# One more x tile of block 1 transposed by DMA instead of TensorE, and one cast of the head in two halves

## The chip, the core and the metric

The kernel runs on one core of a Trainium2 chip. A core has TensorE (PE; its weight loads are shown as PEld), VectorE (DVE), ScalarE (ACT), GpSimd (POOL) and SyncE (SP), which run their own instruction streams and wait for each other by semaphores, and 16 DMA engines. The metric is the device time of one execution in microseconds (us).

## The reference

x is 16 x 512 x 768, w1 768 x 3072, b1 3072, w2 3072 x 768, all float32. What is computed:

```
y = np.matmul(x, w1) + b1
y = 0.5 * y * (1.0 + erf(y / np.sqrt(2.0)))
return np.matmul(y, w2)
```

## The kernel before

**Tiling.** The 8192 rows of x are cut into eight blocks (sb) of 1024 rows; a block has 8 row tiles t of 128 rows. The first product runs with the 768 (k) on the partitions, so a block's x is needed transposed: `XTs[sb]` holds, for row half a (0: tiles 0 to 3, 1: tiles 4 to 7) and k chunk c (0 to 5), 128 x 512 values in fp16. Both products use a 2x2 Strassen-Winograd scheme with seven products p1 to p7. For the first one A11 and A12 are the lower and upper three k chunks of row half 0, and A21 and A22 those of row half 1. The sums of x (`x_sums`, L321) are S1 = A21 + A22 (k = 0), S2 = S1 - A11 (k = 1), then A11 - A21 (k = 2) and A12 - S2 (k = 3), all on DVE.

**Units and periods.** A unit of the first product, `Unit1` for (sb, k), makes 256 of the 3072 hidden values for one block: seven products of three matmuls of 512 columns, 21 matmuls. `period(i, j, fill)` (L666) interleaves unit i with the end of unit j before it: p1(i) into bank bX and its copy to bY (`copy_xy`, ACT, L606); p7(j) into bY and an add on DVE (L613); p5(i) into bW and a copy (ACT, L626); p3(j) into bZ and an add (DVE, L641); p6(i) into bY, and a copy of bY to bZ (for block 0 and even units of block 1 on DVE, L659); right_done(j), a GELU on ACT (L404); p4(j) into bY and its GELU (ACT, L409); p2(i) into bX and its GELU (ACT, L409). Banks bX and bY exist twice, bW and bZ once. Between these calls `fill(slot)` is called with slots 1 to 6, and hangs in the work beside the matmuls: loads, sums, transposes.

**The order of units** at the start is written out by hand in `seq` (L818): units 0 to 6 of block 0, then (1,0), (1,1), (1,2), (0,7) and so on. A unit's place in it is `pos`. The first two are computed in the head with plain matmuls.

**The head** (L713 to L816). SP loads x tiles 0 to 3 of block 0 in float32, then the first two column chunks of w1 in two halves (L723). For each of the four tiles DVE casts it to fp16 (L746), PE transposes six 128 x 128 pieces into the bank bT (`transpose_pe`, L311, the transposes are L313), ACT copies them to XTs[0] (L315; for tile 3 in two halves, `copy_halves`, L307, L309), and some dummy matmuls (`spin`, L737) follow. DVE then casts the w1 chunks in three instructions (L754: two of 384 columns from the first half, one of 768 from the second), and the plain matmuls (L762) begin: three into bX and three into bY with the lower k chunks, then the same with the upper ones.

**x of block 1.** POOL loads its eight tiles with a cast to fp16 (`load_next_x`, L824, issued at L299), in the order 0, 4, 1, 5, 2, 6, 3, 7, between loads of weight tiles 4, 5 and 6 (L222). `transposes_a(pos)` (L850), called in slot 5 of pos 1 to 4, transposes tiles pos - 1 and pos + 3 by DMA on SP's queue (`transpose_dma`, L304), but not those in `X1_PE` (L845), which `fill_a` (L855) transposes on PE in a slot of a pos given by `X1_AT` (L846): tile 3 in slot 2 of pos 5, tile 7 in slot 1 of pos 6. In slot 5 of pos 7, SP stores the weight tiles 0 to 6 with their sums to DRAM (`keep`, L224, issued at L225, times in `KEEP`, L848), behind the transposes on the same queue. The sums of x of block 1 are queued at pos 5 (columns 0 to 255 of k = 0, 1), pos 6 (columns 256 to 511 of k = 0, 1) and pos 7 (k = 2, 3); unit (1,0), at pos 7, is the first to use XTs[1]. `prep_wt` (L227) queues the sums of a weight tile on DVE for the unit behind; all these sums run at L191.

Of the kernel before, what the change touches and what calls it, by code (L numbers as in the profile page):

```python
# [10 lines left out]
P = 128  # L11
# [11 lines left out]
def kernel(  # L23
# [8 lines left out]
    nc = tc.nc  # L32
    B, M, K = x.shape
# [6 lines left out]
    KQ = K // P // 2  # L40
# [48 lines left out]
    def cut(off, n, pattern=None, **dims):  # L89
        ap = arena[:, off:off + n]  # L90
        return ap.rearrange(pattern, **dims) if pattern else ap
# [94 lines left out]
    with tc.manual_schedule():  # L186
# [103 lines left out]
        xhs = {}  # L290

        def xh_of(sb, t):
            if sb < ONE:
                return cut(sb * GR + GR // 2 + t * K, K)
            return xh_late[t % 3]
# [8 lines left out]
        def transpose_dma(sb, t):  # L304
            nc.sync.dma_start_transpose(out=xT_of(sb, t), in_=xhs[t])

        def copy_halves(out, in_):  # L307
            for c in (slice(0, KQ), slice(KQ, 2 * KQ)):
                nc.scalar.copy(out=out[:, c, :], in_=in_[:, c, :])  # L309

        def transpose_pe(sb, t, copy=nc.scalar.copy):  # L311
            for kc in range(2 * KQ):
                nc.tensor.transpose(out=bT[t % 2][:, kc, :], in_=xhs[t][:, kc * P:(kc + 1) * P],  # L313
                                    identity=ident[:])
            copy(out=xT_of(sb, t), in_=bT[t % 2][:])  # L315
# [397 lines left out]
        xf = cut(GR, 8 * K).bitcast(FP32).rearrange("p (t k) -> p t k", t=4)  # L713
# [23 lines left out]
        def spin(n):  # L737

            for k in range(n):
                nc.tensor.matmul(out=(bX[1], bY[1])[k % 2][:], lhsT=zero[:, 0, 0:P], rhs=zero[:, 0, :],  # L740
                                 start=True, stop=True, skip_group_check=True)

        spin(9)
        for t in range(4):
            xhs[t] = xh_of(0, t)
            nc.vector.tensor_copy(out=xhs[t], in_=xf[:, t, :])  # L746
            transpose_pe(0, t, copy_halves if t == 3 else nc.scalar.copy)
            if t == 0:
                nc.tensor.transpose(out=bW[:, 0:2 * NH], in_=bf, identity=idf[0:2 * NH, 0:2 * NH])
                nc.scalar.copy(out=b1t[:], in_=bW[:, 0:2 * NH])  # L750
            spin(2)
# [15 lines left out]
        def plain_done(n, row, side):  # L767
            nc.scalar.activation(out=Gs[0][side][:, n, row, :], in_=banks[n, row][side][:, 0:RH],
                                 func=GELU, bias=b1t[:, 2 * n + side:2 * n + side + 1])
# [72 lines left out]
            if pos in w2_at_pos:  # L842
                load_w2(*w2_at_pos[pos])

        X1_PE = (3, 7)  # L845
        X1_AT = ((5, 2), (6, 1))  # L846

        KEEP = {at[1, 0]: range(7), at[0, 7] + 1: (7,), at[0, 8]: (8,), at[0, 9]: (9,), at[0, 10]: (10,), at[0, 11]: (11,)}  # L848

        def transposes_a(pos):  # L850
            for t in (pos - 1, pos + 3):
                if t not in X1_PE:
                    transpose_dma(1, t)

        def fill_a(pos, slot):  # L855
            if pos == 2 and slot == 1:
                plain(1, 1, 1, 1, bottom)
                plain_done(1, 1, 1)
            if (pos, slot) in X1_AT:
                transpose_pe(1, X1_PE[X1_AT.index((pos, slot))])  # L860
            if pos == at[1, 0] - 1 and slot == 2:
# [267 lines left out]
```

## Time and profile before

| what | value |
|---|---|
| median of 4 runs | 853.23 us (852.84 to 853.58) |
| the profiled execution | 853.01 us, span 851.2 us |
| granted TensorE clock | 1.0 |
| PE busy | 844.6 us, 99% of the span |
| DVE, ACT, POOL busy | 78%, 49%, 10% |
| transposes on PE (L313) | 60: six for each of the eight tiles of block 0 and of tiles 3 and 7 of block 1 |
| DMA transposes on SP (L305) | 54, six of them for block 1 |

The span runs from the first to the last instruction of the program; the execution's own time has 1.8 us more around it. A line of the timeline gives the start and the length in us, the engine, the line of the code, the operation with what it writes and reads, the number of merged instructions, and in brackets the idle time of the engine just before it with what ended it. A matmul's length contains its drain, which the next one overlaps; starts tell the rate. A DMA's line on SP is the time of its issue, not of the transfer; the time from issue to landing is a figure of its own. Line numbers are those of the program above.

### The profile page before, as it was taken

The page shows a single profiled execution, that of the slowest core. Times are in us where ns is not written, and L with a number is a line of the kernel's source. Part 1 is how long each engine was busy: PE and PEld are TensorE (multiplying, and loading weights), DVE is VectorE, ACT ScalarE, POOL GpSimd, SP SyncE. Part 2 cuts the span into 40 slices and gives each one's busy share as a digit, 9 for nine tenths or more (in the row PEclk, how much of TensorE's full clock was granted, in tenths as well). Part 3 has the DMA queues.
Part 4 walks back from the last instruction along what each step waited for, and adds up shares of the span by engine and source line. Part 5 has one row for each costly group of instructions (what it writes and reads, how often), then busy time and mean ns, then how long its engine had stood idle before and what let it go on. Part 6 is the DMA issues. An engine that isn't in the chain of part 4 may idle for free.

```text
span 851.2 us, 16487 instructions
## 1 busy us (share of the span) xinstructions
PE 844.6 (99%) x6432; PEld 568.7 (67%) x6432; DVE 667.4 (78%) x1126; ACT 421.3 (49%) x686; POOL 83.8 (10%) x135
## 2 busy tenths in 40 slices
PE   8999999999999999999999999999999999999998
PEld 5444445687544897448974499645995469944798
DVE  4766678786657998579976799668996689956998
ACT  4777762122277512783148722487216771267611
POOL 5021100002100002000020000210002100010000
PEclk9999999999999999999999999999999999999999
DMA  9998687649999599987999689995999959984398
GB/s 224 193 277 187 159 167 255 256 190 221 231 326 216 191 324 369 319 166 234 341 365 299 130 286 333 362 269 136 318 342 342 285 120 331 352 310 173 100 309 285
DMA packets 143522, 219.05 MB, mean 257 GB/s; under 512 B 61756, under 2 KB 84724, under 8 KB 143444
## 3 DMA queue, kind: packets, MB, share of 16 engines
q1 hardware_dynamic: 117824, 179.74, 66.9%
q0 software_dynamic: 25440, 38.15, 20.6%
q8 instruction: 50, 0.82, 0.4%
q14 instruction: 28, 0.23, 0.1%
q10 hardware_dynamic: 180, 0.11, 0.0%
HBM read 180.30 MB, written 47.87 MB: 268 GB/s over the span
## 4 chain that ended last, share of the span: by engine, by line
PE 98%; DMA 1%; ACT 1%; DVE 0%; issue 0%; SPq 0%; ACTq 0%
PE bY L388 21%; PE bY L493 15%; PE bX L388 14%; PE bX L493 10%; PE bW L388 7%; PE bZ L388 7%; PE bZ L493 5%; PE bW L493 5%; PE bY L432 5%; PE bW L432 2%; PE bX L432 2%; PE bZ L432 2%; PE bY L580 1%; PE bX L580 1%; DMA arena<-in_x_dram 1%; PE bX L762 0%
## 5 line engine op out<-in xcount | busy, mean ns | idle before, releaser
L191 DVE TENSOR_TENSOR arena<-arena 128x768 f16<-128x768 f16 (+4 forms) x630 | 403.8, 672 | 8.1 <-PE bW L432 1.1
L388 PEld LDWEIGHTS <-arena 128*128 128x128 f16 x1974 | 192.5, 98 | 223.9
L493 PEld LDWEIGHTS <-arena 128*128 128x128 f16 x3528 | 292.1, 98 | 8.4 <-issue 0.4
L388 PE MATMUL bY<-arena 128*128 128x512 f16 x846 | 214.4, 379 | 0.0
L613 DVE TENSOR_TENSOR arena<-bY,arena 128x512 f32<-128x512 f32 (+1 forms) x102 | 69.4, 681 | 127.1 <-PE bY L388 90.4
L493 PE MATMUL bY<-arena 128*128 128x192 f16 x1500 | 138.3, 246 | 0.0
L388 PE MATMUL bX<-arena 128*128 128x512 f16 x564 | 138.2, 379 | 0.0
L606 ACT COPY bY<-bX 128x512 f32<-128x512 f32 (+1 forms) x143 | 78.6, 550 | 119.4 <-DVE arena L542 82.0
L404 ACT ACTIVATE arena<-arena,b1t 128x1024 f16<-128x1024 f32 x94 | 108.1, 1150 | 53.8 <-DVE arena L641 53.8
L626 ACT COPY arena<-bW 128x512 f32<-128x512 f32 (+1 forms) x147 | 81.1, 552 | 90.7 <-PE bW L493 43.9
L493 PE MATMUL bX<-arena 128*128 128x192 f16 x1020 | 93.1, 246 | 0.1
L641 DVE TENSOR_TENSOR arena<-bZ,arena 128x512 f32<-128x512 f32 (+1 forms) x102 | 69.3, 680 | 20.9 <-PE bZ L388 18.2
L388 PE MATMUL bW<-arena 128*128 128x512 f16 x282 | 76.2, 379 | 0.0
L388 PE MATMUL bZ<-arena 128*128 128x512 f16 x282 | 76.2, 379 | 0.0
L432 PEld LDWEIGHTS <-arena 128*128 128x128 f16 x528 | 51.6, 98 | 34.1 <-issue 0.2
L525 POOL DMA_DIRECT2D out_dram<-arena x42 | 30.6, 729 | 407.4 <-DVE arena L637 371.3
L409 ACT ACTIVATE arena<-bX,b1t 128x512 f16<-128x512 f32 x94 | 64.0, 681 | 10.0 <-PE bX L388 10.0
L409 ACT ACTIVATE arena<-bY,b1t 128x512 f16<-128x512 f32 x94 | 63.4, 674 | 0.0
L657 ACT COPY bZ<-bY 128x512 f32<-128x512 f32 (+1 forms) x54 | 29.0, 537 | 65.6 <-DVE arena L641 31.4
L299 POOL DMA_DIRECT2D arena<-in_x_dram x60 | 32.6, 550 | 248.1 <-DMA arena<-arena 139.3
L493 PE MATMUL bZ<-arena 128*128 128x192 f16 x504 | 48.4, 246 | 0.0
L493 PE MATMUL bW<-arena 128*128 128x192 f16 x504 | 48.4, 246 | 0.0
(60 smaller groups left out, 400.2 us busy)
## 6 DMA issues: line engine op xcount, KB each, us to landing
arena<-w2s SPq DMA_DIRECT2D x294, 288.0 KB, 4.7
arena<-w1s SPq DMA_DIRECT2D x72, 672.0 KB, 7.1
out_dram<-arena POOLq DMA_DIRECT2D x42, 384.0 KB, 7.4
w2s<-arena SPq DMA_DIRECT2D x49, 288.0 KB, 3.6
arena<-in_x_dram POOLq DMA_DIRECT2D x60, 192.0 KB, 7.0
w1s<-arena SPq DMA_DIRECT2D x12, 672.0 KB, 5.5
arena<-in_w_dram POOLq DMA_DIRECT2D x17, 384.0 KB, 8.8
out_dram<-arena SPq DMA_DIRECT2D x17, 384.0 KB, 3.6
```

The source lines that it names most:

```text
L191: nc.vector.tensor_tensor(out=o, in0=a, in1=b, op=op)
L299: nc.gpsimd.dma_start(out=xhs[t], in_=xr[:, sb * 8 + t, :])
L388: nc.tensor.matmul(out=dst[:, 0:RH], lhsT=w1_op(self.wt, slot)[:, c, :], rhs=a[:, c, :], start=first and c == 0, stop=c == self.C - 1, ski ...
L404: nc.scalar.activation(out=self.G[1][:, hi, :, :], in_=self.tmp, func=GELU, bias=b1t[:, 2 * hi + 1:2 * hi + 2])
L409: nc.scalar.activation(out=self.G[0][:, hi, row, :], in_=bank[:, 0:RH], func=GELU, bias=b1t[:, 2 * hi:2 * hi + 1])
L432: nc.tensor.matmul(out=dst[:, 0:N2], lhsT=a, rhs=w[:, :, c, :], start=first and c == 0, stop=c == self.C - 1, skip_group_check=True)
L493: nc.tensor.matmul(out=dst[:, t * N4:(t + 1) * N4], lhsT=a, rhs=w[:, c, :], start=first and c == 0 and t == ts[0], stop=c == NQ - 1, skip_ ...
L525: eng.dma_start(out=orr[:, s0:s0 + 2, right * N2:(right + 1) * N2], in_=self.dst[:, r].rearrange("p t h n -> p t (h n)"))
L606: nc.scalar.copy(out=bY[u.g % 2][:, 0:u.F], in_=bX[u.g % 2][:, 0:u.F])
L613: nc.vector.tensor_tensor(out=u.c22(), in0=bY[u.g % 2][:, 0:u.F], in1=w[:, 0:u.F], op=ADD)
L626: nc.scalar.copy(out=w[:, 0:u.F], in_=bW[:, 0:u.F])
L641: nc.vector.tensor_tensor(out=u.c12(), in0=bZ[:, 0:u.F], in1=w[:, 0:u.F], op=ADD)
```

## The change

The list of tiles that PE transposes for block 1 loses tile 3, which so goes to `transpose_dma` at pos 4, behind tile 6 and ahead of the keep stores. Tile 7 stays on PE, at the same place. In the head, the cast of x row tile 3 becomes two casts of 384 columns each; the transposes and the two half copies behind it are as before.

```diff
+        KH = KQ * P
...
         for t in range(4):
             xhs[t] = xh_of(0, t)
-            nc.vector.tensor_copy(out=xhs[t], in_=xf[:, t, :])
+            if t < 3:
+                nc.vector.tensor_copy(out=xhs[t], in_=xf[:, t, :])
+            else:
+                nc.vector.tensor_copy(out=xhs[t][:, 0:KH], in_=xf[:, t, 0:KH])
+                nc.vector.tensor_copy(out=xhs[t][:, KH:K], in_=xf[:, t, KH:K])
             transpose_pe(0, t, copy_halves if t == 3 else nc.scalar.copy)
...
-        X1_PE = (3, 7)
-        X1_AT = ((5, 2), (6, 1))
+        X1_PE = (7,)
+        X1_AT = ((6, 1),)
```

KQ is 3 and P is 128, so KH is 384.

## The prediction

> **What bounds the kernel now.** I read the page's busy table first, then the chain that ended last, then the timeline of the two places that the diff touches.
>
> ```profile
> PE 844.6 (99%) x6432; PEld 568.7 (67%) x6432; DVE 667.4 (78%) x1126; ACT 421.3 (49%) x686; POOL 83.8 (10%) x135
> ...
> PE 98%; DMA 1%; ACT 1%; DVE 0%; issue 0%; SPq 0%; ACTq 0%
> ```
>
> TensorE is busy for 844.6 of 851.2 us, and 98% of the chain is matmuls. Its idle time lies almost wholly in the first 10.4 us; behind that a wait of PE is a rare thing of 0.1 to 0.3 us. So work taken off PE is worth its time, unless an engine that was just in time before is now just too late. The whole question is which of those is near.
>
> **Part 1: the six transposes of tile 3 leave PE.** The timeline of units (0,5) and (0,6), PE alone:
>
> ```profile
> 35.12 0.81 PE L388 MATMUL bW<-arena 128*128 128x512 f16 x3
> 35.77 0.50 PE L313 MATMUL bT<-ident,arena 128*128 128x128 f16 x6
> 36.10 0.81 PE L388 MATMUL bZ<-arena 128*128 128x512 f16 x3
> ...
> 39.34 0.81 PE L388 MATMUL bY<-arena 128*128 128x512 f16 x3
> 39.99 0.50 PE L313 MATMUL bT<-ident,arena 128*128 128x128 f16 x6
> ```
>
> The columns are start, span, engine, line. Three matmuls of 512 columns take 0.65 us from start to start (35.12 to 35.77). The six transposes of tile 3 hold PE from 35.77 to 36.10: 0.33 us (the 0.50 counts the last one's drain, which the next matmul overlaps). Removed: 0.33 us of PE, and one ACT copy of 0.81 us (the bT copy at 36.47), which lies in 1.09 us of ACT's idle time and is worth nothing. The six for tile 7 (39.99) stay.
>
> What is late next? DVE, in the same stretch:
>
> ```profile
> 36.59 1.15 DVE L191 TENSOR_TENSOR arena<-arena 128x384 f16<-128x384 f16 x3 [0.51 <-DMA arena<-in_w_dram]
> 37.65 0.68 DVE L641 TENSOR_TENSOR arena<-bZ,arena 128x512 f32<-128x512 f32 x1
> 38.44 0.70 DVE L659 COPY bZ<-bY 128x512 f32<-128x512 f32 x1
> ```
>
> DVE waited until 36.59 for a load of w1 (weight tile 6, for prep_wt), not for PE. The three sums, L641 and the copy bZ<-bY (L659) follow without a gap, so the copy ends at 39.14 whether PE is earlier or not. Behind it waits p7 of unit (0,5), the matmuls into the same bY at 39.34: they overwrite what the copy reads. Elsewhere in this trace PE starts 0.05 us after such a copy (L654 ends at 302.48, PE goes on at 302.53). So p7 can start at 39.19, not at 39.34 - 0.33 = 39.01: of the 0.33 us **0.15 us stays** and 0.18 becomes a wait on DVE.
>
> Does the 0.15 us survive? ACT's chain L404, L409, L409, L606 starts at 38.37 from that L641 and does not move; L606, which p6 of (0,6) waits for, ends at 41.15, and PE wants it at 41.62 - 0.15 = 41.47. The copy of tile 7 stays at 41.08 to 41.89, so the sum S1 (k = 0 of x_sums, columns 256 to 511) stays at 41.92; it reads row block 1, tiles 4 to 7, and not tile 3. From there L641, L404, L409, L409 and L606 end at 45.91, PE could go on at 45.96, and p6 of (1,0) wants 46.15 - 0.15 = 46.00. It just fits. Behind that the waits shrink again, and the rest of the program is moved by 0.15 us as a whole.
>
> **Part 2: a seventh DMA transpose on SP.** It is issued behind that of tile 6 and ahead of keep(0):
>
> ```profile
> 36.84 1.24 SPq L305 DMA_TRANSPOSE arena<-arena  x1
> ...
> 38.17 2.39 SPq L225 DMA_DIRECT2D w1s<-arena  x1
> ```
>
> Its source, x tile 3, has landed by 32.5 (the trace's landing of that load), so it starts at 36.84 + 1.24, some 38.10. Added on SP: one issue of 1.2 us (median of L305: 1.228) to 5.7 us (the longest, for tile 1, with the queue full). The seven or eight keep stores queued behind it move by 1.2 to 2.4 us. The first one landed at 43.4 and its slot is reloaded at 51.1, when POOL is released by PE: 7.7 us of cover, so nothing.
>
> Tile 3 is due when PE starts p1 of unit (1,0), the first reader of A11: 43.56 - 0.15 = 43.41, so a landing by 43.36, which is 5.26 us after the issue. S2 (k = 1), its other reader, runs on DVE at 43.79 and is due only before p6. How long does a transpose take from issue to landing?
>
> ```profile
> DMA to landing us min/median/max: 2.7/5.3/10.9
> ```
>
> Bounds: 2.7 us (landing 40.8) and 10.9 us (49.0). I take the row next to it, tile 6, one place ahead in the same queue: 5.0 us, so 43.1, in time by 0.3 us. Two things say that this is rather too long. Tile 6 stood behind five others, and from about 38.5 to 40.9 the DMA engines moved next to nothing: the packet records have a 16 KB fetch of PE's instructions on queue q8 from 38.17 to 40.18, 2.0 us where most of its kind take 0.9 to 1.0, and the transposes stood still meanwhile. And nothing else loads the queues there: the last weight load landed at 36.56. With 12 PE instructions fewer (six weight loads, six matmuls) the fetch comes about 1 us later and may hold tile 3 instead: then it lands about 1.6 us after the fetch's end, as tile 6 did (40.18 to 41.79), so at 39.15 + 2.0 + 1.6 = 42.75. Still in time.
>
> The Trainium skill speaks against this part. Its page "VectorE: DVE Perf Modes", section "Rules for kernel authors", would transpose 128x128 on TensorE where PSUM will do as destination, and by DMA otherwise; section "The three transpose paths" prices one at 390 ns there and 1309 ns by DMA. An estimate by the page: six by DMA are 7.85 us, a landing at 45.95, and PE would lose about 2.4 us against before. The trace has 55 ns of PE for one transpose in a row of six and whole tiles landing in 2.7 us when undisturbed, so the sum goes by the trace.
>
> **Part 3: the cast of x row tile 3 in two halves.** The head's timeline:
>
> ```profile
> 8.36 0.92 DVE L746 CAST arena<-arena 128x768 f16<-128x768 f32 x1 [0.42 <-DMA arena<-in_x_dram]
> 9.49 0.80 DVE L754 CAST arena<-arena 128x384 f16<-128x384 f32 x2 [0.21 <-DMA arena<-in_w_dram]
> 11.08 0.56 DVE L754 CAST arena<-arena 128x768 f16<-128x768 f32 x1 [0.79 <-DMA arena<-in_w_dram]
> ...
> 10.41 0.81 PE L762 MATMUL bX<-arena 128*128 128x512 f16 x3
> 11.05 0.81 PE L762 MATMUL bY<-arena 128*128 128x512 f16 x3
> ...
> 11.70 0.81 PE L762 MATMUL bX<-arena 128*128 128x512 f16 x3
> ```
>
> The nearest rows for a half are the two w1 casts of 128x384, 0.47 and 0.40 us with starts 0.40 apart. The halves would end at about 8.8 and 9.23 (9.28 before). The last three transposes then start at 9.28 instead of running in a row of six from 9.34, and end at 9.62 instead of 9.84; ACT's first half copy, which began 0.04 after them, and the first matmul come 0.22 earlier, at 10.19. But the second half of these matmuls, at 11.70, reads the third w1 cast, which waits for its load until 11.08 and ends at 11.64; its weight load starts at 11.69. Before, PE was busy until that very moment; now it would be done at 11.48 and wait. **Worth 0.00 us**: the w1 load hides it. The bounds: 0.28 us gained, if that load came as much earlier (the first matmul can go no earlier than the first w1 cast at 9.96 lets it); and 0.92 us lost, if each half took as long as the whole cast, since the second half of the matmuls then moves to 12.62.
>
> **The sum.** 0.15 us off PE, 0 in the head, 0 for SP: the profiled execution goes from 853.01 to 852.86 us (its span from 851.2 to 851.1). The median of the four runs, 853.23, lies 0.22 above it, so I forecast **853.1 us**. A measurement of this kernel can tell about 0.2%, 1.7 us, from no change; this is a tenth of that.
>
> **The rivals.**
> - *The whole gain.* Speaks for it: DVE's late start hangs on one load's landing (36.56), and 0.18 us earlier would free all 0.33 us, 852.9 us; with the head's 0.28 as well, 852.6. Against: both loads are issued as before, with the same traffic beside them. Chance 0.17.
> - *The gain is eaten whole.* p6 of (1,0) fits by 0.04 us only; if the shifted fetch holds tile 6 so that S1 starts at 42.1 instead of 41.92, that chain ends at 46.15 and the time is 853.2. That the change does nothing looks the same. Chance 0.15.
> - *Tile 3 lands late: slower.* PE itself then waits, in front of p1 of (1,0), with everything queued behind it, and every microsecond counts in full. Break-even is a landing at 43.51, 5.4 us after the issue. For it: the median of this line is 5.3, and tile 2, two places ahead, took 6.0. That row would give 44.07 and PE at 44.12 instead of 43.56: 0.56 us slower, 853.8. The longest row, 10.9, gives 49.0: 5.5 us slower, 858.7. Over 0.2% begins at a landing of 45.2, 7.1 us. Against: the long ones ran beside loads of x and w1 or stores, which are absent here. Chance 0.23, of which 0.05 is over 0.2%.
>
> The forecast has 0.45.
>
> **The numbers.** The range reaches from all gains, 853.23 - 0.61 with the 0.39 by which the runs lay under their median, 852.2, to the head's bound, 853.23 + 0.92 with the 0.35 above, 854.5, which takes in tile 3 landing like tile 2. Beyond it lie the very late landings and a measurement that drifts. Faster by over 0.2%: no case gives it, 0.01. Slower by over 0.2%: 0.05 and 0.01 for what I do not see, 0.06. Within: 0.93.
>
> **What would show it.** PE: 54 transposes on L313 instead of 60 and no gap between bW and bZ in unit (0,5); then a wait of about 0.18 us before p7 of (0,5), ended by L659. If that wait is absent, PE keeps 0.33. SP: 55 transposes, the seventh starting near 38.1; its landing against 43.4 decides the slower rival, and PE idle before p1 of (1,0) would be its mark. Head: first matmul near 10.2, then idle before the second half, which still starts at 11.7. The prediction is wrong if the second half moves, if PE waits over 0.2 us anywhere in units (0,5) to (1,1) for something else, or if a stall appears later in the program that 0.15 us does not explain.

## The result

The changed kernel is slower: a median of 853.73 us (852.99 to 855.57, 41 runs) against 852.84 us (852.10 to 853.91, 61 runs), ratio 1.0011 with a 95% interval of 1.0006 to 1.0015. That is 0.9 us lost, between 0.5 and 1.3. I had forecast 0.15 us gained. The time lies in my range, and the loss is smaller than the 0.2% that I had set as the bound, but over so many runs it is clear, and it has the other sign.

### The profile page after: what moved, and what is told of

Its sections match the earlier page's. It is cut to its first block, busy times and chain, and to the rows that moved or that the text cites. A ratio compares the mean times of both kernels' runs of the same rounds, so it can differ in the third digit from the quotient of the medians.

```text
span 852.8 us, 16476 instructions
## 1 busy us (share of the span) xinstructions
PE 845.0 (99%) x6426; PEld 568.8 (67%) x6426; DVE 667.8 (78%) x1127; ACT 420.6 (49%) x685; POOL 83.6 (10%) x135
## 4 chain that ended last, share of the span: by engine, by line
PE 97%; DMA 2%; SPq 0%; DVE 0%; issue 0%
PE bY L390 21%; PE bY L495 15%; PE bX L390 14%; PE bX L495 10%; PE bZ L390 7%; PE bW L390 7%; PE bZ L495 5%; PE bW L495 5%; PE bY L434 5%; PE bZ L434 2%; PE bW L434 2%; PE bX L434 2%; DMA arena<-in_w_dram 2%; PE bY L582 1%; PE bX L582 1%; PE bX L768 0%
## 5 line engine op out<-in xcount | busy, mean ns | idle before, releaser
L390 PEld LDWEIGHTS <-arena 128*128 128x128 f16 x1974 | 192.5, 98 | 226.1 <-DMA arena<-in_w_dram 2.1
L390 PE MATMUL bY<-arena 128*128 128x512 f16 x846 | 214.4, 379 | 0.0
L390 PE MATMUL bX<-arena 128*128 128x512 f16 x564 | 138.4, 379 | 1.6 <-DMA arena<-in_w_dram 1.6
L643 DVE TENSOR_TENSOR arena<-bZ,arena 128x512 f32<-128x512 f32 (+1 forms) x102 | 69.3, 679 | 21.0 <-PE bZ L390 18.2
L390 PE MATMUL bW<-arena 128*128 128x512 f16 x282 | 76.2, 379 | 0.0
L390 PE MATMUL bZ<-arena 128*128 128x512 f16 x282 | 76.2, 379 | 0.0
L659 ACT COPY bZ<-bY 128x512 f32<-128x512 f32 (+1 forms) x54 | 29.0, 537 | 65.4 <-DVE arena L643 32.3
```

The source lines that it names most:

```text
L390: nc.tensor.matmul(out=dst[:, 0:RH], lhsT=w1_op(self.wt, slot)[:, c, :], rhs=a[:, c, :], start=first and c == 0, stop=c == self.C - 1, ski ...
L643: nc.vector.tensor_tensor(out=u.c12(), in0=bZ[:, 0:u.F], in1=w[:, 0:u.F], op=ADD)
```

## The profile after

The profiled execution took 854.58 us with a span of 852.8 us; it lies 0.85 us above its median, so what is lost shows larger in it than it is on average. Lines of the code are 2 to 6 higher than before: L388 is now L390, L313 is L315, L659 is L661, and the w1 cast of the head, L754, is L760. The busy table and the engines' shares of the chain:

```profile
PE 845.0 (99%) x6426; PEld 568.8 (67%) x6426; DVE 667.8 (78%) x1127; ACT 420.6 (49%) x685; POOL 83.6 (10%) x135
...
PE 97%; DMA 2%; SPq 0%; DVE 0%; issue 0%
```

TensorE has six matmuls and six weight loads fewer, but is 97% of the chain instead of 98, and DMA 2% instead of 1: a transfer of some 8 us has come into the chain. Where it sits is told by the chain in order of time (start, length, what):

```profile
50.03 0.66 PE bZ L390 x3
50.69 0.28 issue
50.97 7.74 DMA arena<-in_w_dram
58.72 0.05 issue
58.76 0.82 PE bX L390 x3
```

At 50.97 POOL issues the load of weight tile 7 (L222), released by PE; it lands at 58.72, and PE goes on at 58.76 with p1 of unit (0,7). The two timelines of PE there, before and after:

```profile
55.22 1.46 PE L388 MATMUL bY<-arena 128*128 128x512 f16 x6
56.51 1.46 PE L388 MATMUL bX<-arena 128*128 128x512 f16 x6
57.80 0.81 PE L388 MATMUL bY<-arena 128*128 128x512 f16 x3
```

```profile
55.05 1.46 PE L390 MATMUL bY<-arena 128*128 128x512 f16 x6
56.34 0.81 PE L390 MATMUL bX<-arena 128*128 128x512 f16 x3
58.76 0.82 PE L390 MATMUL bX<-arena 128*128 128x512 f16 x3 [1.61 <-DMA arena<-in_w_dram]
```

Before, p2 of the last unit and p1 of (0,7) ran as six matmuls in a row: p1 began at 57.16, 0.34 after the load's landing at 56.82. Now p1 could have begun at 56.98 and begins at 58.76: 1.78 us of wait (1.61 in the bracket, which counts from the drain of the last matmul). The rest of the two profiles agrees: the first unit's matmuls begin 0.17 later (22.01 against 21.84, the head), the saved transposes bring 0.33, and 0.17 - 0.33 + 1.78 is 1.62; the spans differ by 1.57.

Why does the load land 1.9 us later, when it was issued 0.17 earlier? POOL's issue of it, before and after:

```profile
51.14 0.83 POOL L222 DMA_DIRECT2D arena<-in_w_dram  x1 [25.47 <-PE bZ L388]
```

```profile
50.97 0.83 POOL L222 DMA_DIRECT2D arena<-in_w_dram  x1 [25.52 <-PE bZ L390]
```

SP's queue, before and after:

```profile
38.17 9.10 SPq L225 DMA_DIRECT2D w1s<-arena  x7
```

```profile
36.76 1.24 SPq L305 DMA_TRANSPOSE arena<-arena  x1
...
38.09 3.12 SPq L305 DMA_TRANSPOSE arena<-arena  x1
...
41.30 7.20 SPq L225 DMA_DIRECT2D w1s<-arena  x7
```

The seventh transpose holds SP for 3.12 us, and the seven keep stores begin 3.1 us later. Their first packets come at 42.33 instead of 41.16, their last ones end at 55.30 instead of 53.58 (the trace's packets of 5376 bytes). The DMA view from 50 to 52 us, right when the load has been issued, before and after (queue, packets, MB, share; then size and median us to landing of the two loads issued there, tile 7 and a piece of w2):

```profile
q1 hardware_dynamic: 173, 0.84, 103.1%
...
arena<-in_w_dram POOLq DMA_DIRECT2D x2, 384.0 KB, 6.2
```

```profile
q1 hardware_dynamic: 174, 0.85, 104.1%
...
arena<-in_w_dram POOLq DMA_DIRECT2D x2, 384.0 KB, 8.3
```

All that moves is SP's queue q1, the stores, at 0.42 MB per us; of POOL's queue q0 not a packet moves yet. The load's first packet comes at 53.22 before and at 54.42 after, close to the end of the stores in both. So 1.2 of the 1.9 us lie ahead of the first packet. The other 0.7 lie behind it (4.3 us from the first packet to the landing, 3.6 before), and no run here shows why.

## The experiments

Theory S: the seventh transpose pushes the stores back, the load of weight tile 7 gets the DMA engines only as they end, and PE, which had 0.34 us to spare there, waits for it. Rivals: the head's two casts cost the time (H); the load is late for another reason, such as the transposes themselves (L); PE's own work decides (P). Ratios are to the kernel before, run beside.

| run | ratio (95% interval) | load of tile 7: issued, first packet, landed | PE's wait before p1 of (0,7) |
|---|---|---|---|
| before | | 51.14, 53.22, 56.82 | 0 |
| changed | 1.0011 (1.0006 to 1.0015) | 50.97, 54.42, 58.72 | 1.61 |
| tile 3 alone | 1.0015 (1.0006 to 1.0024) | 50.78, 54.14, 58.47 | 1.56 |
| head alone | 1.0000 (0.9991 to 1.0009) | 51.43, 53.25, 56.42 | 0 |
| changed, two stores late | 1.0001 (0.9993 to 1.0010) | 50.66, 52.20, 55.56 | 0 |
| before, one store more | 1.0014 (1.0005 to 1.0023) | 50.56, 53.73, 58.05 | 1.36 |
| all eight by DMA | 1.0030 (1.0018 to 1.0041) | 52.83, 55.38, 59.26 | 0.30 |
| three tiles by PE | 1.0006 (0.9997 to 1.0015) | 51.27, 52.80, 56.39 | 0 |
| changed, PE transposes too | 1.0013 (1.0004 to 1.0022) | 51.59, 54.16, 58.37 | 0.65 |
| before, two stores late | 1.0004 (0.9996 to 1.0013) | 51.33, 52.87, 56.25 | 0 |

Issue, packet, landing and wait are those of one profiled execution each, the waits as the timeline's bracket gives them. The room between landing and first use varies too: 0.34 us before, 1.02 with the head alone, whose stores and loads stand in the same order.

**Tile 3 by DMA alone.**

```diff
-        X1_PE = (3, 7)
-        X1_AT = ((5, 2), (6, 1))
+        X1_PE = (7,)
+        X1_AT = ((6, 1),)
```

> Only tile 3 by DMA, the cast in the head whole. Theory S (the seventh transpose pushes the keep stores back by about 1.6 us, the load of weight tile 7 queues behind them, and PE waits for it ahead of p1 of (0,7)): as the changed kernel, 0.5 to 1.3 us slower than before, with PE idle 1 to 2 us ahead of p1 of (0,7). Rival H (the two half casts delay the head): no loss, 0.15 us faster than before.

853.76 us against 852.89: the whole loss is in this half of the change, with the same wait.

**The head's two casts alone.** The rest of the diff, with the two lines above as before.

> Only the cast in two halves, tile 3 transposed by PE. Theory S: within 0.2 us of before; the load of weight tile 7 lands near 56.8 and PE does not wait for it. Rival H: 0.5 to 1.3 us slower, all of it before the second half of the first plain matmuls.

852.92 us against 852.89: nothing lost or gained, within 0.8 us. With the whole loss in the run before it, H falls. The head of this run's profile shows what ate the earlier start (timeline; the plain matmuls, L762, are L768 here):

```profile
10.22 0.82 PE L768 MATMUL bX<-arena 128*128 128x512 f16 x3
...
11.36 0.56 DVE L760 CAST arena<-arena 128x768 f16<-128x768 f32 x1 [0.64 <-DMA arena<-in_w_dram]
...
11.98 0.39 PE L768 MATMUL bX<-arena 128*128 128x512 f16 x1 [0.29 <-DVE arena L760]
```

PE waits in front of the second half of the plain matmuls for the third w1 cast, which waits for its load.

**The changed kernel with the stores of tiles 5 and 6 behind that of tile 8.**

```diff
-        KEEP = {at[1, 0]: range(7), at[0, 7] + 1: (7,), at[0, 8]: (8,),
+        KEEP = {at[1, 0]: range(5), at[0, 7] + 1: (7,), at[0, 8]: (8, 5, 6),
```

> The changed kernel, with the keep stores of weight tiles 5 and 6 moved behind that of tile 8, so that five stores and not seven stand ahead of the load of weight tile 7. Theory S: that load lands by 56.8, PE does not wait ahead of p1 of (0,7), and the 0.15 us of the transposes is kept: 0.1 to 0.35 us faster than before, some 1.0 us faster than the changed kernel. Rival L (the load is slow for another reason than the stores, for example the transposes themselves): 0.5 to 1.3 us slower than before, as the changed kernel.

853.09 us against 852.89, and 0.67 below the run with tile 3 alone beside it. The interval alone reaches from 0.6 us gained to 0.9 lost; the profile tells more: the wait ahead of p1 of (0,7) is gone. The DMA view from 50 to 52 us, where the stores have now ended:

```profile
q1 hardware_dynamic: 4, 0.01, 1.3%
...
arena<-in_w_dram POOLq DMA_DIRECT2D x2, 384.0 KB, 5.4
```

The load's first packet comes 1.54 us after its issue (2.08 before, 3.45 in the changed kernel) and it lands 1.1 us before PE wants it. L falls: the seven transposes are all there. The hoped gain is not to be seen. In this profile PE waits elsewhere, for 0.28 of the 0.33 us: p7 of (0,5) begins at 38.86, 0.05 after the copy bZ<-bY ends.

```profile
36.27 1.14 DVE L191 TENSOR_TENSOR arena<-arena 128x384 f16<-128x384 f16 x3 [0.61 <-DMA arena<-in_w_dram]
37.33 0.68 DVE L643 TENSOR_TENSOR arena<-bZ,arena 128x512 f32<-128x512 f32 x1
38.11 0.70 DVE L661 COPY bZ<-bY 128x512 f32<-128x512 f32 x1
```

```profile
37.72 1.03 PE L390 MATMUL bX<-arena 128*128 128x512 f16 x4
38.86 0.81 PE L390 MATMUL bY<-arena 128*128 128x512 f16 x3
```

**The kernel before with one store more.** Weight tile 0 is stored a second time, to a place that nothing reads (w1x, a DRAM tile of the same size).

```diff
                 for n in KEEP.get(pos, ()):
                     keep(n)
+                    if n == 0:
+                        nc.sync.dma_start(out=w1x[:], in_=wts[0])
```

> The kernel before, with one store more: weight tile 0 is stored a second time to a place that nothing reads, behind the first of the seven stores. 672 KB at the 0.42 MB per us that the stores reach is 1.6 us. Theory S: the load of weight tile 7 lands about 1.6 us later, of which the 0.3 us of slack before p1 of (0,7) covers a part: 1.3 us slower than before, with no DMA transpose added. Rival L: no difference to before.

854.07 us against 852.89: 1.2 us lost (0.4 to 2.0), where 1.3 was expected, with no transpose added and PE's work as before (two lines more, so L388 is L390 here too).

```profile
58.10 0.82 PE L390 MATMUL bX<-arena 128*128 128x512 f16 x3 [1.36 <-DMA arena<-in_w_dram]
```

So what the stores on SP's queue still have to move decides when the load on POOL's queue lands, whatever put it there.

**All eight tiles by DMA.**

```diff
-        X1_PE = (7,)
-        X1_AT = ((6, 1),)
+        X1_PE = ()
+        X1_AT = ()
```

> The changed kernel with tile 7 transposed by DMA as well: eight transposes on SP, none of block 1 on PE, and another 0.33 us of PE work gone. Theory S: the stores begin 0.7 to 1.6 us later still, the load of weight tile 7 lands near 60 instead of 58.7, and PE waits for it: 1.5 to 3 us slower than before, so 0.6 to 2 us slower than the changed kernel, though PE has less to do. Rival P (PE's own work counts and the loss is a single event): as the changed kernel or 0.3 us better.

855.20 us against 852.73: 2.5 us lost, within the expectation, though PE has 0.66 us less to do than before. But not by the wait that I had expected:

```profile
PE bY L390 <- DVE bZ L661: 2.2, 2, 1.7
...
PE bX L390 <- DMA arena<-in_w_dram: 0.3, 1, 0.3
```

The columns are the total, the number of waits and the longest. On DVE:

```profile
43.81 0.56 DVE L191 TENSOR_TENSOR arena<-arena 128x768 f16<-128x768 f16 x1 [2.58 <-DMA arena<-arena]
44.28 0.68 DVE L643 TENSOR_TENSOR arena<-bZ,arena 128x512 f32<-128x512 f32 x1
45.07 0.70 DVE L661 COPY bZ<-bY 128x512 f32<-128x512 f32 x1
```

The transpose of x tile 7 lands later than ACT's copy of it came, so the sum S1 starts at 43.81 and not at 41.92, L643 and the copy bZ<-bY stand behind it on DVE, and PE waits 1.7 us for that copy; the load of weight tile 7 is itself issued later, since PE releases it, and only 0.3 us of its lateness is left. That S had the size right is luck: most of the loss came at a place that it did not have.

**Three tiles by PE.** The kernel before, with tile 2 transposed by PE as well.

```diff
-        X1_PE = (3, 7)
-        X1_AT = ((5, 2), (6, 1))
+        X1_PE = (2, 3, 7)
+        X1_AT = ((4, 4), (5, 2), (6, 1))
```

> The kernel before with tile 2 transposed by PE as well as 3 and 7, so five transposes by DMA. Theory S: the load of weight tile 7 lands earlier than 56.8, PE does not wait there, and the six transposes cost 0.33 us of PE: 0.2 to 0.4 us slower than before. Rival L (the load's landing does not hang on the queue ahead of it): the landing stays at 56.8.

853.27 us against 852.73: 0.5 us, with an interval that holds no change, so the time alone is inconclusive. The profile: the units' first 400 matmuls take 87.67 us from the first one's start instead of 87.33, the 0.34 us of six transposes, and no wait ahead of (0,7). The load lands at 56.39, 0.4 earlier than in the profile of before, but no earlier than with the head alone (56.42), where the stores are as before: here they have ended at 52.18, and the load takes 5.1 us from its issue. So this run does not tell S from L.

**The changed kernel with the PE transposes of tile 3 made as well,** into a bank that nobody reads, with no copy.

```diff
             if (pos, slot) in X1_AT:
                 transpose_pe(1, X1_PE[X1_AT.index((pos, slot))])
+            if (pos, slot) == (5, 2):
+                for kc in range(2 * KQ):
+                    nc.tensor.transpose(out=bT[0][:, kc, :], in_=xhs[3][:, kc * P:(kc + 1) * P],
+                                        identity=ident[:])
```

> The changed kernel, with the six PE transposes of tile 3 made as well, into a bank that nobody reads, at their old place. PE has its 0.33 us back, the DMA side is that of the changed kernel. Theory S: the load's landing decides, so PE waits 0.3 us less ahead of p1 of (0,7) and the time is that of the changed kernel, 0.9 us slower than before. Rival P: 0.3 us slower than the changed kernel.

853.60 us against 852.73: 0.9 us lost (0.3 to 1.9), the changed kernel's loss, for 0.33 us more of PE work. Such an interval cannot tell 0.3 us; the profiles say more. From the first unit's matmul to the end the two profiles take 830.85 and 830.80 us. PE's waits:

```profile
PE bX L390 <- DMA arena<-in_w_dram: 0.6, 1, 0.6
PE bY L390 <- DVE bZ L661: 0.5, 1, 0.5
```

What PE loses earlier, to transposes or to DVE, it waits less for the load. P falls with this and with the run of all eight by DMA, 2.5 us slower than before with less PE work: as long as PE waits for a transfer in the end, work ahead of that wait is free.

**The kernel before with the same two stores late.** The diff of `KEEP` above, on the kernel before.

> The kernel before, with the keep stores of weight tiles 5 and 6 moved behind that of tile 8, as in the run of the changed kernel with late stores. Theory S: the load of weight tile 7 was in time already, so no difference to before (within 0.2 us). Rival M (moving these stores is worth time by itself): as much faster than before as the changed kernel with late stores is faster than the changed kernel.

853.28 us against 852.73, no difference within the interval, and the middle of it is above 1. Late stores bring nothing where PE was not waiting. Whether they cost 0.2 to 0.5 us later on stays open by the times; the profiles show no such cost: from the first unit's matmul to the end this one takes 829.53 us, before 829.40, and the head alone, where no store moved, 829.56. No version here beats the kernel before.

## Why the prediction was wrong

- **The step that failed** is in part 2: "The seven or eight keep stores queued behind it move by 1.2 to 2.4 us. The first one landed at 43.4 and its slot is reloaded at 51.1 [...] 7.7 us of cover, so nothing." In the sum it stands as "0 for SP"; in the profile of the changed kernel it is 1.78 us of wait. I asked who waits for a store's landing, and the answer, the reload of its slot, is right: that load was issued as early as ever. I did not ask what else the stores' 4.8 MB hold up. They fill the DMA engines from 41 to 54 us, the reload is the next transfer behind them, and it had 0.34 us to spare before PE, which the prediction does not work out. The late stores (wait gone) and the extra store (loss made without the change) show it.
- The rival with the other sign had the wrong transfer: tile 3 itself was in time. It landed at 42.76, where I had 43.1 or, with the fetch in its way, 42.75, and PE did not wait in front of p1 of (1,0). That 42.75 fits so well is luck: the fetch did not come 1 us later, and its 2.0 us are not the time in which the transposes stood still (last section). A landing too late, paid in full by PE, was the right shape, but for another load.
- The issue on SP took 3.12 us, inside my 1.2 to 5.7, and no run shows why an issue takes so long; the stores moved by 3.1 and not 1.2 to 2.4, but their data by 1.2 to 1.7.
- The 0.33 us of PE was right: bW to bZ in unit (0,5) is 35.28 to 35.93 now, no gap (timeline of the changed kernel, PE; the tile 7 transposes are still at their place).

```profile
35.28 0.81 PE L390 MATMUL bW<-arena 128*128 128x512 f16 x3
...
35.93 0.81 PE L390 MATMUL bZ<-arena 128*128 128x512 f16 x3
...
39.17 0.81 PE L390 MATMUL bY<-arena 128*128 128x512 f16 x3
...
39.82 0.50 PE L315 MATMUL bT<-ident,arena 128*128 128x128 f16 x6
```

  The 0.18 us that DVE was to take of it came neither always nor never: 0 in the changed kernel's profile, where the head ran 0.17 later, 0.28 with the late stores, where it ran 0.43 earlier. DVE's start hangs on a load that does not move with PE, as I had it.
- The head's 0.00 us agrees with the run of the head alone, whose interval of 0.8 us either way cannot tell 0.2. The reason given shows in that run's profile. In the changed kernel's it does not: the second half cast took 0.65 us, the first plain matmul came at 10.56 instead of 10.41, and PE did not wait for the third w1 cast.
- The Trainium skill's rule in "VectorE: DVE Perf Modes", "Rules for kernel authors", to transpose on TensorE, is on the side of the result, but the page's price is not what decided: by the prediction's estimate from it tile 3 would have landed at 45.95, and it landed at 42.76.

## What to carry to other kernels

A transfer moved on a queue is to be followed not only to whoever waits for it, but to the next transfer that needs the same DMA engines, and that one's landing is to be set against the moment when the bounding engine wants its data. In this kernel, at 99% of TensorE, 0.33 us of work taken off it was worth nothing, because a load behind it lost more than the 0.34 us that it had to spare. Before moving work onto DMA, list the loads of the next 20 us with their slack.

## What the runs showed of the hardware

- Bulk stores on SP's queue hold up a load on POOL's. Its first packet came 1.5 us after the issue in the three profiles where the last store's packet was out before it (the changed kernel and the one before with late stores, three tiles by PE), and 1.8 to 3.5 us after it in the other seven, between 0.9 and 0.2 us ahead of the end of the stores. The Trainium skill, "DMA: Bandwidth & Descriptors", section "Rules for kernel authors", says that DMAs issued by different engines run on the same 16 DMA engines and interleave. That the two queues share the engines agrees with the load's waiting; interleaving is not to be seen here: in this stretch the load did not get a share beside the stores, but its first packets as they ran out. Why is open.
- The DMA transposes stop beside instruction fetches. In the changed kernel an 8 KB fetch ran from 37.82 to 38.18 us and one of 16 KB from 38.14 to 40.11. The transposes moved next to nothing from 38.5 to 39.1 and from 39.5 to 40.8, ran in between, and tiles 2, 6 and 3 landed one after the other at 41.11, 41.83 and 42.76. I had the 16 KB fetch come 1 us later, with 12 instructions fewer ahead of it; it came at the same time as before (38.17). It does not always last 2.0 us there: in five of the ten profiles it took 1.05 or 1.06. That the fetches are what stops the transposes is not shown.
- A cast of half of x tile 3 (128x384), with POOL issuing DMAs all the while, took 0.34 to 0.74 us in the profiles with the change to the head, and the whole one (128x768) 0.56 to 0.92 us in the others. The spread is as large as what the split could give. It goes with POOL: the halves of 0.49 us and more and the wholes of 0.64 us and more are those in which POOL began a new issue 0.2 to 0.5 us after the cast's start; in the others none began later than 0.1 us into it. Why is open.
